# Weaving a layer's dependent attention steps between its dense products on TensorE

## The chip, the cores and the metric

The kernel runs on one core of one Trainium2 chip. The metric is the device time of one execution in microseconds (us); a smaller number is better. Three runs of the kernel before gave 2191.29, 2193.53 and 2195.86 us, so its median is 2193.53 us.

## The reference

One layer of a decoder trunk is computed for 512 positions of width 2048, all in float32. Three groups of heads read the same normed input, and their outputs are put side by side and go through one output projection; a SwiGLU network follows. Cut to what matters here:

```python
h = rmsnorm(x, norm1_g)
(u, v, dq, dk, dv, gq, gk, gv, gr, gcode) = jnp.split(h @ w_in, IN_SPLIT_IDX, axis=-1)
a_out = gmlp_mixer(u, v, ...)          # gelu(u) * (W_s layernorm(gelu(v)) + b), chunks of 128
b_out = diff_attention(dq, dk, dv, ...)  # 6 heads; (softmax(s1) - lam * softmax(s2)) @ v, then rmsnorm
c_out = gla_mixer(gq, gk, gv, gr, gcode, ...)  # 4 heads; gated linear attention, rmsnorm, * silu(r)
x = x + jnp.concatenate([a_out, b_out, c_out], -1) @ w_out
x = x + swiglu(rmsnorm(x, norm2_g), w_ffn_in, w_ffn_out)
return rmsnorm(x, final_g)
```

## The kernel before

Matrices lie in tiles of 128 partitions, and float32 products are made of three products of a reduced form: every operand is split into a high part (cast by ScalarE) and a low part (subtracted by VectorE), and `mm3` (L115) multiplies high by high, high by low and low by high. These are the dense products. Weights come in by DMA from SyncE's queue in halves of 128x1024 and are split by `split_w` (L105) or in `xstat` (L145).

The work around the change has this order in the program. First the value projection of the gMLP group (`xstat` "a") and the root mean square. Then the small spatial products `sp` (L262). Then the GLA values ("c", two blocks of columns), and the gate codes (`gct`, L287). Then 28 outputs of 128 columns each by `wstat` (L192): queries and keys of the four GLA heads (`wsg`), the gates (`wsr`), queries and keys of the six attention heads (`wsd`), and the gMLP's u (`wsu`). Each is 16 tiles deep, so 48 dense products of 512 columns. Between them stand the values of the differential attention ("b", L448: 384 products of 384 columns).

Two kinds of dependent chains hang on these. `gla(h, q, k)` (L309) takes a gate product `z`, three activations with different tables (L317 to L319), and then nine levels hs = 1, 2, 4, ... 256: exponentials on ScalarE (L356, L360), products on VectorE (L361, L362), four small matmuls `A` on TensorE (L341), a masked copy back (L343), and the running sums that the next level needs (L376, L378). Outputs `o` (L396), a norm, and transposes `ox` (L412) end a head. `attn(h)` (L453) makes stacked operands (L465 to L470), and for four blocks of queries scores `sc` (L481), softmax pieces, the difference of the two (L499 to L502) and transposes `pt` (L506); then `do` (L513), a norm, and transposes `dx` (L526).

Last, the gMLP gate (L537, L538) and the split of the mixed activations into `mxs` (L543 to L545) feed the output projection `wo_half` (L601). `mxs` takes the memory of `xs`, the split input, once the last `wstat` has read it. The output projection begins with the first half of the depth of four outputs (LEAD) and then takes their second halves.

Small matmuls and transposes share four PSUM banks (pool `sml`), dense products another four (`big`). The order of the instructions on each engine is not that of the program text: the compile's scheduler lets each engine take what it expects to be ready, by its own estimates, so on TensorE too the small steps stand where the scheduler put them.

Of the kernel before, what the change touches and what calls it, by code (L numbers as in the profile page):

```python
# [8 lines left out]
F32 = mybir.dt.float32  # L9
# [7 lines left out]
P = 128  # L17
# [32 lines left out]

@with_exitstack
def trunk_kernel(
# [22 lines left out]
    act, dve, pe, pool = nc.scalar, nc.vector, nc.tensor, nc.gpsimd  # L75
# [69 lines left out]
    def xstat(src, width, blocks, evac, name, first=False):  # L145
        for b, (c0, cw) in enumerate(blocks):
# [4 lines left out]
            for kn in steps:  # L151
# [40 lines left out]
    def wstat(j, name, halves=(0, 1)):  # L192
        b = big.tile([P, T], F32, tag="b", name=f"ws{name}")
        for hf in halves:
            wh, wl = split_w(wst[j, hf].rearrange("p k c -> p (k c)"), 1024, f"{name}_{hf}")
            for kk in range(8):
                k = 8 * hf + kk
# [61 lines left out]
    for g in range(4):  # L259
        pg = ps(f"sp{g}")  # L260
        for n in range(4):
            pe.matmul(pg[:, n * P:n * P + P], lhsT=va[:, n, g * P:g * P + P], rhs=spw[:, g], start=True, stop=True)  # L262
        dve.scalar_tensor_tensor(out=mix[:, g].rearrange("p (a b) -> p a b", b=P),
                                 in0=pg.rearrange("p (a b) -> p a b", b=P), scalar=lngs[:, g:g + 1],
                                 in1=spbb[:, g:g + 1].to_broadcast([P, 4, P]), op0=ALU.mult, op1=ALU.add)
# [19 lines left out]
    pt = ps("gct")  # L285
    for i in range(4):
        pe.transpose(pt[:16, i * P:i * P + P], gcs[:, i], ident)  # L287
    for r in (0, 32, 64):
        dve.tensor_copy(gcf[r:r + 16], pt[:16])
    act.copy(gct[:96], gcf[:96])  # L290
    dve.tensor_sub(gct[32:64], gcf[32:64], gct[32:64].bitcast(F32))
# [17 lines left out]
    def gla(h, q, k):  # L309
# [12 lines left out]
        dve.memset(suf, 0.0)  # L322

# [24 lines left out]
        hs = 1  # L348
        while hs <= 256:
# [12 lines left out]
            dve.tensor_mul(v(c)[:, :, 1], v(c)[:, :, 1], v(qh)[:, :, 1])  # L362
            if hs <= 64:
# [11 lines left out]
            if hs < 256:  # L375
                dve.tensor_add(v(suf)[:, :, 0], v(suf)[:, :, 0],  # L376
                               v(pre)[:, :, 1, hs - 1:hs].to_broadcast([DK, nb, hs]))
                dve.tensor_add(v(pre)[:, :, 1], v(pre)[:, :, 1],  # L378
                               v(pre)[:, :, 0, hs - 1:hs].to_broadcast([DK, nb, hs]))
            hs *= 2  # L380
        blk = {(0, 1): 4, (2, 3): 5, (0, 2): 6, (0, 3): 7, (1, 2): 8, (1, 3): 9}
# [46 lines left out]
    gla(3, *gq[3])  # L428

# [23 lines left out]
    def attn(h):  # L453
# [6 lines left out]
        q, k = qk  # L460
        quads = []
        for m in range(2):
            own, other = slice(64 * m, 64 * m + 64), slice(64 - 64 * m, 128 - 64 * m)
            qh, ql, kk = (stacked(f"{n}{h}_{m}") for n in ("qh", "ql", "kk"))
            act.copy(kk[own], k[own])  # L465
            dve.tensor_sub(kk[other], k[own], kk[own].bitcast(F32))
            for r in (own, other):
                act.copy(qh[r], q[own])
            for r in (own, other):
                dve.tensor_sub(ql[r], q[own], qh[own].bitcast(F32))  # L470
            quads.append((qh, ql, kk))
# [57 lines left out]
    for h in range(6):  # L529
        attn(h)  # L530
# [537 lines left out]
```

## Time and profile before

| | us |
|---|---|
| median of three runs | 2193.53 |
| the profiled execution, its own time | 2196.51 |
| its span, first to last instruction | 2194.7 |
| TensorE busy with matmuls (PE) | 2153.8 (98%) |
| VectorE busy (DVE) | 1522.8 (69%) |
| ScalarE busy (ACT) | 1010.5 (46%) |
| mean granted TensorE clock | 0.988 of full speed |

The page shows TensorE near full from end to end, so the few places where it is not are what is to be looked for. The granted clock is 1.00 (2.4 GHz) or 0.50 (1.2 GHz) at any moment; a stretch's mean below 1.00 says how much of it was at the lower level. A matmul's end is modelled, so a wait that is shorter than the modelled end doesn't show as idle time. A busy time alone therefore says less than the step from one start to the next.

### The profile page before, as it was taken

The numbers are of one execution on the slowest core, as the hardware profiler recorded it, in microseconds if no ns is written. First come the engines' busy times: TensorE is split into PE (matmuls) and PEld (weight loads), VectorE is DVE, ScalarE is ACT, GpSimd is POOL, SyncE is SP. The second block draws the span as 40 slices with busy tenths as digits, with TensorE's granted clock in tenths as the row PEclk, the third lists the DMA queues.
The fourth block names the chain that finished last, engine by engine and source line by source line (L and its number), as shares of the span: only waits on it lengthen the run. The fifth ranks groups of instructions, "written<-read, shape, count | busy, mean of one in ns | idle before, by whom it ended". The sixth has DMA issues, their size and how long they took to land.

```text
span 2194.7 us, 37812 instructions
## 1 busy us (share of the span) xinstructions
PE 2153.8 (98%) x15650; PEld 2053.9 (94%) x15650; DVE 1522.8 (69%) x2046; ACT 1010.5 (46%) x1456; POOL 58.7 (3%) x126
## 2 busy tenths in 40 slices
PE   9999999999989999999999999999999999999997
PEld 7988798878879999999999999999999999999987
DVE  6433754376665759777777777777777689888746
ACT  6323555355565546444444444444444634533444
POOL 1000000000001000000000000000000000000000
PEclk9999989999999999999999999999999999999998
DMA  6332121322237774343333333433333654733335
GB/s 204 90 106 96 34 58 46 104 77 77 70 129 240 226 229 160 123 148 117 140 119 133 130 129 117 149 119 122 114 130 119 199 154 141 229 113 103 111 102 179
DMA packets 105260, 284.63 MB, mean 130 GB/s; under 512 B 11216, under 2 KB 42368, under 8 KB 105088
## 3 DMA queue, kind: packets, MB, share of 16 engines
q1 hardware_dynamic: 81728, 236.88, 33.5%
q0 software_dynamic: 6720, 27.53, 3.4%
q10 hardware_dynamic: 16640, 17.80, 2.7%
q8 instruction: 123, 2.02, 0.4%
q14 instruction: 49, 0.40, 0.1%
HBM read 256.74 MB, written 25.43 MB: 129 GB/s over the span
## 4 chain that ended last, share of the span: by engine, by line
PE 93%; DVE 3%; ACT 2%; DMA 1%; issue 1%; SPq 0%; DVEq 0%; ACTq 0%
PE bx L116 7%; PE bx L118 7%; PE bx L117 7%; PE bz L117 4%; PE bz L118 4%; PE bz L116 4%; PE wo L116 3%; PE wo L117 3%; PE wo L118 3%; PE sx L118 2%; PE sx L116 2%; PE sx L117 2%; PE by L116 2%; PE by L118 2%; PE by L117 2%; PE wsd L116 2%
## 5 line engine op out<-in xcount | busy, mean ns | idle before, releaser
L118 PE MATMUL bx<-op,fl 128*128 128x256 f32 x1344 | 378.8, 282 | 0.4 <-DVE fl L659 0.4
L116 PE MATMUL bx<-op,fh 128*128 128x256 f32 x1344 | 379.1, 282 | 0.0
L117 PE MATMUL bx<-op,fh 128*128 128x256 f32 x1344 | 378.5, 282 | 0.0
L658 ACT CAST fh<-s 128x1024 fp32r<-128x1024 f32 x168 | 176.3, 1050 | 267.6 <-PE bx L117 127.1
L659 DVE TENSOR_TENSOR fl<-s,fh 128x1024 fp32r<-128x1024 f32 x168 | 205.4, 1223 | 87.3 <-ACT fh L658 85.2
L118 PEld LDWEIGHTS bx<-op,fl 128*128 128x128 f32 x1344 | 254.0, 189 | 0.6 <-DVE fl L659 0.6
L116 PEld LDWEIGHTS bx<-op,fh 128*128 128x128 f32 x1344 | 254.4, 189 | 0.0
L117 PEld LDWEIGHTS bx<-op,fh 128*128 128x128 f32 x1344 | 254.1, 189 | 0.0
L658 ACT CAST fh<-f 128x1024 fp32r<-128x1024 f32 x126 | 132.2, 1049 | 198.9 <-PE bx L117 72.3
L118 PE MATMUL bz<-op,fl 128*128 128x256 f32 x672 | 189.8, 282 | 0.1
L117 PE MATMUL bz<-op,fh 128*128 128x256 f32 x672 | 189.8, 282 | 0.0
L116 PE MATMUL bz<-op,fh 128*128 128x256 f32 x672 | 189.5, 282 | 0.0
L659 DVE TENSOR_TENSOR fl<-f,fh 128x1024 fp32r<-128x1024 f32 x126 | 154.0, 1222 | 35.0 <-ACT fh L658 35.0
L116 PE MATMUL wo<-mxs,wh_o 128*128 128x256 f32 x512 | 145.6, 284 | 0.0
L117 PE MATMUL wo<-mxs,wh_o 128*128 128x256 f32 x512 | 145.3, 284 | 0.0
L118 PE MATMUL wo<-mxs,wl_o 128*128 128x256 f32 x512 | 145.2, 284 | 0.0
L116 PE MATMUL sx<-fop,wh_s 128*128 128x256 f32 x448 | 127.1, 284 | 2.5 <-ACT wh_s L855 2.5
L118 PEld LDWEIGHTS bz<-op,fl 128*128 128x128 f32 x672 | 127.7, 190 | 0.3 <-DVE fl L659 0.3
L117 PEld LDWEIGHTS bz<-op,fh 128*128 128x128 f32 x672 | 127.8, 190 | 0.0
L116 PEld LDWEIGHTS bz<-op,fh 128*128 128x128 f32 x672 | 127.7, 190 | 0.0
L118 PE MATMUL sx<-fop,wl_s 128*128 128x256 f32 x448 | 127.2, 284 | 0.4 <-DVE wl_s L856 0.4
L117 PE MATMUL sx<-fop,wh_s 128*128 128x256 f32 x448 | 127.1, 284 | 0.0
(439 smaller groups left out, 5941.6 us busy)
## 6 DMA issues: line engine op xcount, KB each, us to landing
f<-wf SPq DMA_DIRECT2D x168, 512.0 KB, 3.8
w_o<-wout SPq DMA_DIRECT2D x32, 512.0 KB, 4.3
w2o<-wout SPq DMA_DIRECT2D x32, 512.0 KB, 4.6
sraw<-wf SPq DMA_DIRECT2D x32, 448.0 KB, 3.8
sw<-wf SPq DMA_DIRECT2D x32, 448.0 KB, 4.2
opd<-tmp POOLq DMA_DIRECT2D x14, 896.0 KB, 4.0
w_d<-wst SPq DMA_DIRECT2D x24, 512.0 KB, 3.3
w_g<-wst SPq DMA_DIRECT2D x16, 512.0 KB, 3.3
```

The costliest lines, as they stand in the source:

```text
L116: pe.matmul(out, lhsT=lh, rhs=rh, start=start, stop=False, skip_group_check=skip)
L117: pe.matmul(out, lhsT=lh, rhs=rl, start=False, stop=False, skip_group_check=skip)
L118: pe.matmul(out, lhsT=ll, rhs=rh, start=False, stop=stop, skip_group_check=skip)
L658: act.copy(wh, a)
L659: dve.tensor_sub(wl, a, wh.bitcast(F32))
```

## The change

TensorE's calls go through a small object `Queue`. It keeps a running estimate of TensorE time, and from the spatial products to the first half of the output projection every matmul is marked to stay in the order of the program. That order is now written by hand: the dependent chains (spatial products, gate codes, four GLA heads, six attention heads) are generators, and a `tick` ahead of each dense step of `mm3` runs those chains whose delay has passed; a `yield 3.4` asks, by that estimate, for 3.4 us of other TensorE work behind a step. The GLA level's factors are now made one level ahead of their product. The GLA heads follow one another from the gate outputs on (`wsr`) and no longer from the queries and keys of the third head. In the attention, the first probability is no longer scaled by its sum (the norm behind takes the sum in), and two of the stacked operands are copied by ScalarE instead of subtracted by VectorE. The gMLP gate, the split into `mxs` and the first halves of the output projection now stand behind the last `wsu` and inside the kept order.

```diff
+class Queue:
+
+
+
+    def __init__(self, tc):
+        self.tc, self.held, self.t, self.chains = tc, False, 0.0, []
...
+    def note(self, ins, out, rhs):
+        n = 1
+        for x in out.shape[1:]:
+            n *= x
+        self.t += max(0.112, 0.006 + n * 0.00044) if rhs.dtype == F32R else 2 * max(0.111, n * 0.00083)
+        if self.held:
+            self.tc.keep_in_program_order(ins)
...
+    def begin(self, chain, delay):
+        self.chains.append([chain, self.t + delay])
+
+    def tick(self, until=None):
+        for c in list(self.chains):
+            while c in self.chains and (until or self.t >= c[1]):
+                try:
+                    c[1] = self.t + next(c[0])
+                except StopIteration:
+                    self.chains.remove(c)
...
+    pe = Queue(tc)
...
         for hf in halves:
             wh, wl = split_w(wst[j, hf].rearrange("p k c -> p (k c)"), 1024, f"{name}_{hf}")
             for kk in range(8):
+                pe.tick()
                 k = 8 * hf + kk
                 c = slice(kk * P, kk * P + P)
...
+    def spatial():
+        for g in range(4):
+            pg = ps(f"sp{g}")
+            for n in range(4):
+                pe.matmul(pg[:, n * P:n * P + P], lhsT=va[:, n, g * P:g * P + P], rhs=spw[:, g], start=True, stop=True)
...
+            yield 2.0
+
+    pe.held = True
+    pe.begin(spatial(), 14.0)
...
+    pe.begin(codes(), 4.0)
...
+        def factors(hs):
...
+        c = factors(1)
+        yield 5.0
+        hs = 1
+        while hs <= 256:
+            nxt = factors(2 * hs) if hs < 256 else None
             if hs <= 64:
                 pick(c, hs, f"{h}_{hs}")
...
+            c = nxt
             hs *= 2
+            yield 3.4
+        far[0] = h + 1
+        while gated[0] < (4 if h < 2 else 6):
+            yield 1.0
...
-    gq = [gla_qk(0), gla_qk(1)]
+    gated = [0]
+
+    def silu(i0, i1):
+        act.activation(mix[:, MIXC + i0:MIXC + i1], mix[:, MIXC + i0:MIXC + i1], AF.Silu)
+        gated[0] = i1
+
+    def heads():
+        for h in range(4):
+            while len(gq) <= h or far[0] < h:
+                yield 1.0
+            pe.begin(gla(h, *gq[h]), 2.0)
+            yield 1.0
+
+    far = [0]
+    gq = [gla_qk(0)]
+    pe.begin(heads(), 0.0)
     for i in range(C_FULL):
         b = wstat(8 + i, f"r{i}")
         dve.tensor_mul(mix[:, MIXC + i], b, rs1)
-        act.activation(mix[:, MIXC + i], mix[:, MIXC + i], AF.Silu)
-    gla(0, *gq[0])
-    gq.append(gla_qk(2))
-    gla(1, *gq[1])
-    gq.append(gla_qk(3))
-    for i in range(C_FULL, 6):
-        act.activation(mix[:, MIXC + i], mix[:, MIXC + i], AF.Silu)
-    gla(2, *gq[2])
-    gla(3, *gq[3])
+    silu(0, C_FULL)
+    for h in range(1, 4):
+        gq.append(gla_qk(h))
+    silu(C_FULL, 6)
...
+            act.copy(qh[own], q[own])
             act.copy(kk[own], k[own])
+            dve.tensor_sub(ql[own], q[own], qh[own].bitcast(F32))
             dve.tensor_sub(kk[other], k[own], kk[own].bitcast(F32))
-            for r in (own, other):
-                act.copy(qh[r], q[own])
-            for r in (own, other):
-                dve.tensor_sub(ql[r], q[own], qh[own].bitcast(F32))
+            act.copy(qh[other], q[own])
+            act.copy(ql[other], ql[own].bitcast(F32))
             quads.append((qh, ql, kk))
+        yield 9.0
...
-            dve.reciprocal(st[:, 6:8], st[:, 4:6])
-            dve.tensor_mul(st[:, 7:8], st[:, 7:8], neglam)
-            dve.tensor_scalar_mul(pr[0][:, :w], pr[0][:, :w], st[:, 6:7])
+            dve.reciprocal(st[:, 6:7], den[:, 4 + qt:5 + qt])
+            dve.scalar_tensor_tensor(out=st[:, 7:8], in0=st[:, 6:7], scalar=neglam, in1=den[:, qt:qt + 1],
+                                     op0=ALU.mult, op1=ALU.mult)
...
+        p0, p1 = scores(0), scores(1)
+        yield 5.0
+        p2 = scores(2)
+        yield 4.0
+        turn(0, p0)
+        turn(1, p1)
+        yield 3.0
+        p3 = scores(3)
+        yield 3.0
+        turn(2, p2)
+        yield 5.0
+        turn(3, p3)
+        yield 2.0
...
+        dve.scalar_tensor_tensor(out=ds[:, 4:8], in0=den[:, 0:4], scalar=128 * EPS, in1=den[:, 0:4],
+                                 op0=ALU.mult, op1=ALU.mult)
+        dve.tensor_add(ds[:, 0:4], ds[:, 0:4], ds[:, 4:8])
+        act.activation(ds[:, 0:4], ds[:, 0:4], AF.Sqrt, scale=1.0 / 128)
         dve.reciprocal(ds[:, 4:8], ds[:, 0:4])
...
+        pe.begin(attn(h, *attn_qk(h)), 0.0)
...
+    ugs = []
     for g in range(4):
         b = wstat(24 + g, f"u{g}", (1, 0) if g == 3 else (0, 1))
-        ug = t2(f"ug{g}")
-        dve.tensor_mul(ug, b, rs1)
-        act.activation(ug, ug, AF.Gelu_apprx_tanh)
-        dve.tensor_mul(mix[:, g], mix[:, g], ug)
+        ugs.append(qk_tile(f"ug{g}"))
+        dve.tensor_mul(ugs[g], b, rs1)
+
+    def gate():
+        for g in range(4):
+            act.activation(ugs[g], ugs[g], AF.Gelu_apprx_tanh)
+            dve.tensor_mul(mix[:, g], mix[:, g], ugs[g])
 
 
     mxs = operand("mxs")
-    for k in ORDER:
-        hi, lo = (mxs[w][SLOT[k] // 4][:, SLOT[k] % 4] for w in range(2))
-        act.copy(hi, mix[:, k])
-        dve.tensor_sub(lo, mix[:, k], hi.bitcast(F32))
+
+    def split_mix(ks):
...
+    def wo_half(n, th, hf):
...
+    split_mix(ORDER[:11])
+    wo_half(0, 0, 0)
+    gate()
+    split_mix(ORDER[11:15])
+    for n in range(1, LEAD):
+        wo_half(n, 0, 0)
+    pe.drain()
+    pe.held = False
+    split_mix(ORDER[15:])
...
             if th == 0 and n == LEAD:
-                for m in range(LEAD):
-                    wo_half(m, 0, 0)
                 for m in range(LEAD):
                     wo_half(m, 0, 1)
```

On TensorE, between the second and the third level of GLA head 0, before (`A0_2`, `A0_4` are the levels' small products, `wsg20` a dense output):

```order
L341 MATMUL A0_2_1635<-c2_0_1630 128x64 x4
L116 MATMUL wsg20_1767<-xs02_103,wh_g20_1_1800 128x512
L117 MATMUL wsg20_1767<-xs12_107,wh_g20_1_1800 128x512
L118 MATMUL wsg20_1767<-xs02_103,wl_g20_1_1801 128x512
L116 MATMUL wsg20_1767<-xs03_104,wh_g20_1_1800 128x512
L117 MATMUL wsg20_1767<-xs13_108,wh_g20_1_1800 128x512
L118 MATMUL wsg20_1767<-xs03_104,wl_g20_1_1801 128x512
L341 MATMUL A0_4_1648<-c4_0_1643 128x64 x4
```

Six dense products stand there (5 to 10 between the other levels of this head). The same place in the changed kernel (`wsr1` is the dense output there; every matmul has the line of the helper):

```order
L67 MATMUL A0_2_1336<-c2_0_1296 128x64 x4
L67 MATMUL wsr1_1319<-xs00_101,wh_r1_0_1322 128x512
L67 MATMUL wsr1_1319<-xs10_105,wh_r1_0_1322 128x512
L67 MATMUL wsr1_1319<-xs00_101,wl_r1_0_1323 128x512
...
L67 MATMUL wsr1_1319<-xs01_102,wh_r1_0_1322 128x512
L67 MATMUL wsr1_1319<-xs11_106,wh_r1_0_1322 128x512
L67 MATMUL wsr1_1319<-xs01_102,wl_r1_0_1323 128x512
L67 MATMUL A0_4_1361<-c4_0_1329 128x64 x4
```

Twelve dense products stand between the two, and 12 to 18 between the levels of all four heads.

On TensorE, the end of the last attention head before (`pt5_3`, `do5`, `dx5` are its last steps, `wo0` the output projection):

```order
L116 MATMUL wsu3_4804<-xs01_102,wh_u3_0_4837 128x512
L117 MATMUL wsu3_4804<-xs11_106,wh_u3_0_4837 128x512
L118 MATMUL wsu3_4804<-xs01_102,wl_u3_0_4838 128x512
L506 MATMUL pt5_3_4578<-ident_510,p5_3_0_4570 128x128 x4
L513 MATMUL do5_4584<-dv_2540,dat5_4491 128x128 x10
L526 MATMUL dx5_4603<-ident_510,don5_4601 128x128 x4
L116 MATMUL wo0_0_4957<-mxs02_4871,wh_o0_00_4960 128x256
```

and in the changed kernel:

```order
L70 MATMUL pt5_3_4702<-ident_510,p5_3_0_4645 128x128 x4
L67 MATMUL wsu2_4692<-xs00_101,wh_u2_0_4695 128x512
...
L67 MATMUL do5_4714<-dv_2238,dat5_4516 128x128 x10
L67 MATMUL wsu2_4692<-xs00_101,wh_u2_0_4695 128x512
...
L70 MATMUL dx5_4762<-ident_510,don5_4733 128x128 x4
L67 MATMUL wsu2_4692<-xs02_103,wh_u2_1_4752 128x512
...
L67 MATMUL wo0_0_4881<-mxs02_4853,wh_o0_00_4884 128x256
```

Nothing dense stood between the three last steps; now 6 products stand ahead of `do5`, 21 ahead of `dx5`, and 66 (the rest of `wsu2` and all 48 of `wsu3`) between `dx5` and `wo0`.

On VectorE, the split of the mixed activations (`mxs1` tiles) in the changed kernel, beside the low parts of the output projection's weights (`wl_o`) and the gate of the last u (`ug3`):

```order
L622 TENSOR_TENSOR don5_4733<-do5_4714,ds5_4727 128x512
L150 TENSOR_TENSOR wl_u3_0_4822<-w_u3_0_4819,wh_u3_0_4821 128x1024
L638 TENSOR_TENSOR ug2_4786<-wsu2_4692,rs1_99 128x512
L150 TENSOR_TENSOR wl_o0_00_4885<-w_o0_00_4882,wh_o0_00_4884 128x1024
L643 TENSOR_TENSOR mix_79<-mix_79,ug2_4786 128x512
L652 TENSOR_TENSOR mxs12_4857<-mix_79,mxs02_4853 128x512 x4
L150 TENSOR_TENSOR wl_o1_00_4932<-w_o1_00_4929,wh_o1_00_4931 128x1024
L652 TENSOR_TENSOR mxs13_4858<-mix_79,mxs03_4854 128x512 x4
L652 TENSOR_TENSOR mxs10_4855<-mix_79,mxs00_4851 128x512 x2
L638 TENSOR_TENSOR ug3_4849<-wsu3_4788,rs1_99 128x512
L652 TENSOR_TENSOR mxs10_4855<-mix_79,mxs00_4851 128x512
L652 TENSOR_TENSOR mxs11_4856<-mix_79,mxs01_4852 128x512 x3
```

Before, eleven of these splits stood ahead of `don5`, in the last head's softmax; now all sixteen stand behind it.

## Rows read from the trace of the kernel before

**Rows 1.** Page, part 1: busy us and share of the span, by engine.
```profile
PE 2153.8 (98%) x15650; PEld 2053.9 (94%) x15650; DVE 1522.8 (69%) x2046; ACT 1010.5 (46%) x1456; POOL 58.7 (3%) x126
```

**Rows 2.** Windows: stretch, length, busy us by engine, clock, DMA share, GB/s.
```profile
120.00:215.00 95.00, 95.00 (x422) 77.91 (x422) 31.84 (x33) 24.95 (x28) 0.00 (x0) 1.00 0.30 99
215.00:295.00 80.00, 77.42 (x419) 65.24 (x418) 54.46 (x116) 47.40 (x92) 1.65 (x8) 0.98 0.17 50
295.00:375.00 80.00, 73.73 (x408) 70.33 (x407) 44.13 (x103) 42.80 (x90) 0.00 (x0) 0.87 0.15 43
440.00:620.00 180.00, 177.44 (x873) 144.30 (x872) 123.63 (x262) 101.20 (x198) 0.00 (x0) 1.00 0.23 77
620.00:637.00 17.00, 8.07 (x39) 7.42 (x38) 9.89 (x20) 9.80 (x17) 0.00 (x0) 0.71 0.10 31
```

**Rows 3.** Waits of TensorE, 0 to 660 us: us in total, times, longest.
```profile
PE pt L506 <- DVE p L502: 7.8, 6, 5.6
PE A L341 <- DVE c L362: 7.0, 5, 2.6
PE dx L526 <- DVE don L522: 3.3, 1, 3.3
```

**Rows 4.** Chain of waits, the gate codes: start us, us, what.
```profile
124.56 0.44 PE gct L287 x4
```

**Rows 5.** Timeline of TensorE, 272 to 276 us: start, us, instruction, count.
```profile
272.34 1.00 PE L341 MATMUL A<-c 96*128 96x64 f32 x8
273.15 0.48 PE L117 MATMUL wsg<-xs,wh_g 128*128 128x512 f32 x1
273.47 0.39 PE L118 MATMUL wsg<-xs,wl_g 128*128 128x512 f32 x1
...
275.09 0.39 PE L116 MATMUL wsg<-xs,wh_g 128*128 128x512 f32 x1
```

**Rows 6.** Timeline of TensorE, 298 to 306 us; in brackets idle before, releaser.
```profile
297.72 0.34 PE L169 MATMUL b<-wh_b,xs 128*128 128x384 f32 x1
...
298.77 0.34 PE L169 MATMUL b<-wh_b,xs 128*128 128x384 f32 x1
298.95 0.33 PE L170 MATMUL b<-wl_b,xs 128*128 128x384 f32 x1
301.02 1.08 PE L341 MATMUL A<-c 96*128 96x64 f32 x8 [1.74 <-DVE c L362]
301.90 0.42 PE L171 MATMUL b<-wh_b,xs 128*128 128x384 f32 x1
```

**Rows 7.** Timeline of ScalarE, 213 to 224 us, head 0 of GLA.
```profile
214.08 1.05 ACT L111 CAST wh_g<-w_g 128x1024 fp32r<-128x1024 f32 x1 [4.52 <-PE wsr L117]
215.03 0.68 ACT L317 ACTIVATE ab<-z,gbs 96x512 f32<-96x512 f32 x1
215.61 0.62 ACT L420 ACTIVATE mix<-mix 128x512 f32<-128x512 f32 x1
216.25 1.28 ACT L318 ACT_TABLE_LOAD   x1
217.54 0.64 ACT L318 ACTIVATE ab<-ab 96x512 f32<-96x512 f32 x1
```

**Rows 8.** Chain of waits, 210 to 245 us: first, fourth and fifth levels of head 0.
```profile
222.46 1.11 PE A L341 x8
...
231.85 0.84 PE A L341 x8
...
234.15 0.84 PE A L341 x8
```

**Rows 9.** Timeline, 618 to 637 us: the tail, TensorE and VectorE.
```profile
621.77 1.23 DVE L112 TENSOR_TENSOR wl_o<-w_o,wh_o 128x1024 fp32r<-128x1024 f32 x1 [0.32 <-ACT wh_o L111]
622.99 1.89 DVE L545 TENSOR_TENSOR mxs<-mix,mxs 128x512 fp32r<-128x512 f32 x3
626.47 1.09 PE L506 MATMUL pt<-ident,p 128*128 128x128 f32 x4 [5.62 <-DVE p L502]
634.62 1.11 PE L526 MATMUL dx<-ident,don 128*128 128x128 f32 x4 [3.31 <-DVE don L522]
635.39 0.56 PE L116 MATMUL wo<-mxs,wh_o 128*128 128x256 f32 x1
```

More of the change, by code (lines that the diff above doesn't have):

```diff
@@ L48, in group_of, with matmul, transpose, drain @@
     return 0 if S0 <= j < S0 + 14 else 1 if S1 <= j < S1 + 14 else None
+class Queue:
[8 more added lines that the diff above has]
+            self.tc.keep_in_program_order(ins)
+    def matmul(self, out, lhsT, rhs, **k):
+        self.note(self.tc.nc.tensor.matmul(out, lhsT=lhsT, rhs=rhs, **k), out, rhs)
+    def transpose(self, out, in_, ident):
+        self.note(self.tc.nc.tensor.transpose(out, in_, ident), out, in_)
+    def begin(self, chain, delay):
[7 more added lines that the diff above has]
+                    self.chains.remove(c)
+    def drain(self):
+        while self.chains:
+            self.tick(True)
 @with_exitstack
@@ L258, in trunk_kernel @@
     dve.memset(one1, 1.0)
[L259 to L265, printed above, removed]
+    def spatial():
[3 more added lines that the diff above has]
+                pe.matmul(pg[:, n * P:n * P + P], lhsT=va[:, n, g * P:g * P + P], rhs=spw[:, g], start=True, stop=True)
+            dve.scalar_tensor_tensor(out=mix[:, g].rearrange("p (a b) -> p a b", b=P),
+                                     in0=pg.rearrange("p (a b) -> p a b", b=P), scalar=lngs[:, g:g + 1],
+                                     in1=spbb[:, g:g + 1].to_broadcast([P, 4, P]), op0=ALU.mult, op1=ALU.add)
+            yield 2.0
+    pe.held = True
+    pe.begin(spatial(), 14.0)
     gv = mix[:, 4:10].rearrange("p a t -> p (a t)").rearrange("p (i c) -> p i c", c=768)
@@ L284, in trunk_kernel, with codes @@
     dve.memset(gcf[:96], 0.0)
[L285 to L291, printed above, removed]
+    def codes():
+        pt = ps("gct")
+        for i in range(4):
+            pe.transpose(pt[:16, i * P:i * P + P], gcs[:, i], ident)
+        for r in (0, 32, 64):
+            dve.tensor_copy(gcf[r:r + 16], pt[:16])
+        act.copy(gct[:96], gcf[:96])
+        dve.tensor_sub(gct[32:64], gcf[32:64], gct[32:64].bitcast(F32))
+        yield 0.0
+    pe.begin(codes(), 4.0)
     def qk_tile(name):
@@ L459, in attn @@
             qk.append(t)
-        q, k = qk
+        return qk
+    def attn(h, q, k):
         quads = []
@@ L529, in trunk_kernel @@
     for h in range(6):
-        attn(h)
+        pe.begin(attn(h, *attn_qk(h)), 0.0)
+    ugs = []
     for g in range(4):
         b = wstat(24 + g, f"u{g}", (1, 0) if g == 3 else (0, 1))
-        ug = t2(f"ug{g}")
-        dve.tensor_mul(ug, b, rs1)
-        act.activation(ug, ug, AF.Gelu_apprx_tanh)
-        dve.tensor_mul(mix[:, g], mix[:, g], ug)
-    mxs = operand("mxs")
-    for k in ORDER:
-        hi, lo = (mxs[w][SLOT[k] // 4][:, SLOT[k] % 4] for w in range(2))
-        act.copy(hi, mix[:, k])
-        dve.tensor_sub(lo, mix[:, k], hi.bitcast(F32))
+        ugs.append(qk_tile(f"ug{g}"))
[4 more added lines that the diff above has]
+            dve.tensor_mul(mix[:, g], mix[:, g], ugs[g])
+    mxs = operand("mxs")
+    def split_mix(ks):
+        for k in ks:
+            hi, lo = (mxs[w][SLOT[k] // 4][:, SLOT[k] % 4] for w in range(2))
+            act.copy(hi, mix[:, k])
+            dve.tensor_sub(lo, mix[:, k], hi.bitcast(F32))
+    wob, wqs = {}, []
+    HALF = (slice(0, TH), slice(TH, T))
+    def wo_half(n, th, hf):
+        hs = HALF[th]
+        if hf == 0:
+            wob[n] = big.tile([P, T], F32, tag="b", name=f"wo{n}_{th}")[:, :TH]
+        wh, wl = split_w(wout[n, hf].rearrange("p k c -> p (k c)"), 1024, f"o{n}_{th}{hf}",
+                         None if hf == 0 or pe.held else wqs[0].tile([P, 1024], F32, tag="raw", bufs=3, name=f"w2o{n}_{th}"))
+        for kk in range(8):
+            pe.tick()
+            i = 8 * hf + kk
+            k = SLOT[ORDER[i]]
+            c = slice(kk * P, kk * P + P)
+            mm3(wob[n], wh[:, c], wl[:, c], mxs[0][k // 4][:, k % 4, hs], mxs[1][k // 4][:, k % 4, hs],
+                i == 0, i == KT - 1)
+    split_mix(ORDER[:11])
[7 more added lines that the diff above has]
+    split_mix(ORDER[15:])
     mp.release()
@@ L598, in trunk_kernel @@
              9: lambda: op_pair(2, b21)}
-    wob, xrs = {}, {}
-    def wo_half(n, th, hf):
-        hs = HALF[th]
-        if hf == 0:
-            wob[n] = big.tile([P, T], F32, tag="b", name=f"wo{n}_{th}")[:, :TH]
-        wh, wl = split_w(wout[n, hf].rearrange("p k c -> p (k c)"), 1024, f"o{n}_{th}{hf}",
-                         None if hf == 0 else wq.tile([P, 1024], F32, tag="raw", bufs=3, name=f"w2o{n}_{th}"))
-        for kk in range(8):
-            i = 8 * hf + kk
-            k = SLOT[ORDER[i]]
-            c = slice(kk * P, kk * P + P)
-            mm3(wob[n], wh[:, c], wl[:, c], mxs[0][k // 4][:, k % 4, hs], mxs[1][k // 4][:, k % 4, hs],
-                i == 0, i == KT - 1)
     def wo_out(n, th):
```

34 lines of the change are left out of this document (20 added, 14 removed).

## The prediction

> **What bounds the kernel now.** I read the page first: TensorE is busy for 2153.8 of 2194.7 us [rows 1], so only a stretch in which it waits or runs at the lower clock can give time back. Then the windows over the part that the change touches [rows 2]. From 120 to 215 us there is nothing to get: 95.00 busy of 95.00, clock 1.00. The GLA heads' 160 us (215 to 375) have 2.6 + 6.3 = 8.9 us idle and a clock of 0.98 and 0.87, that is 1.6 + 10.4 = 12 us of capacity gone at 1.2 GHz. The attention (440 to 620) is idle for 2.6 of 180. The tail (620 to 637) is the worst: 8.9 of 17 idle, clock 0.71, so another 4.9. Idle and slow together make some 37 us. The waits say on what [rows 3]: a transpose for the softmax, a level's product for its factors, the last transposes for the norm, all of them VectorE results at the end of a dependent chain.
>
> A busy time hides short waits, so I set the stage's work against its length. It runs from the gate codes at 124.56 [rows 4] to the first product of the output projection at 635.39 [rows 9]: 510.8 us. One 512-column product takes 0.231: seven steps from 273.47 to 275.09 [rows 5]. There are 28 x 48 = 1344 of them, 311 us. One of 384 columns takes 0.175, six steps from 297.72 to 298.77 [rows 6]; 384 make 67. The small instructions: eight A take 0.81 [rows 5], so 0.10 to 0.11 each up to 128 columns, and 512 of that kind (256 in the GLA levels and their diagonal, 16 at 128 columns included in 272, then 120 `do`, 116 transposes, 4 codes) make 54; 196 wider ones (`o`, `sc`, the last levels, `z`) at 0.17, my estimate between 0.10 and 0.23, make 33. The sum is 465, and the stage loses 510.8 - 465 = 45 us. That is the most the change can give, since it takes no matmul away.
>
> **The change, part by part.** *What stays.* TensorE has the same matmuls in the same forms, and from the first `wo0` product on they come in the order of before. All of it is decided in the stage of 511 us.
>
> *The tail* stands from 626.47 - 5.62 = 620.85 to 635.39 [rows 9], 14.5 us, with 3 us of work in it (four transposes, twenty `do`, four `dx` at 0.105 to 0.11): 11.5 of the 45. Now 6 products stand ahead of `do5` and 21 ahead of `dx5`, 21 x 0.231 = 4.9 us. The norm between the two made TensorE wait for 3.31 us [rows 9], table load included, so it is hidden. What is late next is the split into `mxs`: before, eleven of sixteen ran inside the last softmax; now all follow the norm and wait for `xs`, whose last reader is `wsu3`. On VectorE that is 16 x 0.63 + four weight halves at 1.23 [rows 9] + about four 0.6 products = 17.4 us. The cover from the middle of `wsu3` (the first tiles come free there) to the second halves of the output projection is 5.5 + 4 x 24 x 0.119 = 17 us (a 256-column step taken as half of 0.231 and a little). So VectorE is just full. The first splits are done in time, since the first half of each output needs only eight of them; the third output's low weights stand behind eight splits and the gate, and I make them 0.5 to 1 us late. I take 1; with a VectorE that enters this part 4 us late it is 5.
>
> *The GLA heads and the attention* hold the other 33.5. Of these 21 show as idle or slow under the GLA heads and 2.6 under the attention (above); the hidden 10 I halve between them, an estimate: 26 and 7.5.
>
> *The GLA heads.* Each level's product followed the last by 2.05 to 2.3 us (231.85 to 234.15) [rows 8], which is what the chain of sums, exponentials and products needs, with 5 to 10 products as cover; any late step showed at once, and the clock fell after. Now 12 to 18 products stand there: 12 x 0.231 + 0.81 = 3.6 us, or 15 x 0.175 + 0.81 = 3.4 under "b", 1.1 to 1.3 us more than the chain. One weight split (1.23 [rows 9]) fits into that, and the factors are one level ahead. Each head's start is tighter. From `ab` to the first product took 222.46 - 215.03 = 7.4 [rows 7, 8], with a Silu (0.62) that has moved; so 6.8, plus 0.2 from `z` to ScalarE, plus a weight cast (1.05 [rows 7]) which heads 0 and 1 now have in between: 8.0. Cover: 30 products and the diagonal, 6.9 + 0.8 = 7.7. Late by 0.3, twice. Under head 2 a Silu over two tiles with two table loads stands between levels 4 and 8: 2 x 1.28 + 1.1 = 3.7 against three levels' slack of 3.4, late by 0.3. Head 3 shares ScalarE with the four copies that empty the banks of "b", late by 0.7. With 0.5 per head for what I can't see, 3.6; I take 4.
>
> A row speaks on the table loads: the activation after one starts 0.01 us behind it (216.25 + 1.28 to 217.54) [rows 7]. The Trainium skill (ScalarE: Activation LUTs, "What ACT_TABLE_LOAD costs") counts for every switch, besides the load, a drain of about 1.38 us. No drain shows on this ScalarE, so the trace does not agree. By that rule three loads per head start would be 4.1 us longer for four heads, some 16 us less gain, an estimate from that page; by the row nothing.
>
> *The attention.* VectorE loses the scaling of the first probability (24 instructions) and 12 subtractions, ScalarE gets 12 copies and 4 table loads. Both have room (VectorE 124 of 180, ScalarE 101 of 180 [rows 2]). With about 96 products per head, 22 us, between the steps of two heads, I take 0.7 per head as still lost, over half of what it is now: 4.
>
> *Sum.* 1 + 4 + 4 = 9 of the 45 stay; 36 go. The profiled execution's own 2196.5 becomes 2160.5. The median shown is 3.0 below that execution, so I forecast 2158 us. Unknown from both sides: at best all 45 go (2149); at worst every late step named comes at double and the tail at 5 (-27, 2167).
>
> **The rivals.**
>
> *One order, many stops.* A late step now holds back everything. That it does so is in the trace: at 298.95 `b` products stop, the A at 301.02 waits 1.74 us, and the next `b` product, which needs none of it, runs only behind it [rows 6]. The Trainium skill (TensorE: Matmul & The Clock Gate, "Step-by-step: what each phase is for") says that matmuls stay in program order and only weight loads are pulled ahead; the trace agrees, by those 1.74 us. The written order has some 108 places where a dependent step stands in front of dense work (4 spatial, 1 codes, 48 GLA, 55 attention). 45 / 108 = 0.42 us late at each is the point from which nothing is gained; at 0.6 it is 65 - 45 = 20 slower, 2213. For it: delays come from an estimate, and a wait here measured up to 2.6 [rows 3]. Against: the slack of 1.1 to 1.3 per level above, and that before only 12 waits of these kinds showed [rows 3] with half the cover.
>
> *The GLA's start stays the bound.* ScalarE's queue, not TensorE's order, could set z to first level and the Silu of head 2. If each head is still 3 us late in all and the clock falls after it, 12 of the 26 stay: 2158 + 12 = 2170. For it: 0.87 of the clock sits exactly there. Against: 7.7 of cover to 8.0.
>
> *Dearer table loads.* If a load among more work costs double its 1.28 us [rows 7], three at each head's start are 4 x 3 x 1.28 = 15 us late: 2173. Against: nothing follows the one load in rows 7.
>
> *The splits take the tail's place.* VectorE is full for 17 us; if it comes in late, the first output projection waits 9 to 10 instead of 1: 2167.
>
> *Nothing changes.* If the scheduler's order was already limited by VectorE throughput, waits only move: 2193. Against: VectorE is busy for 0.55 to 0.69 of these windows [rows 2].
>
> **How the numbers follow.** Forecast 0.73 (its own range 2149 to 2167); GLA start 0.11; table loads 0.02; splits 0.06; nothing 0.03; one order 0.05. The measurement of this kernel can tell about 0.2%, 4.4 us. Faster: 0.73 + 0.11 + 0.02 + 0.06 = 0.92; same 0.03; slower 0.05. The range of 8 in 10 reaches from all 45, less 2 for the spread of single runs, to a GLA that stays half late with the table loads: 2147 to 2174.
>
> **What would show it.** Right: the stretch from the gate codes to the first `wo0` product lasts some 475 us instead of 511; the granted clock is 1.00 in all windows between; TensorE's waits for level factors and for `dx` are gone from the list or under 1 us each; level products stand 3.4 to 3.6 us apart. Wrong: a wait of over 1 us at one place in every head; a clock under 1.00 between 215 and 620 us; `wo0` to `wo3` waiting for a split or its weights.

## The result, and the profile after

The changed kernel takes 2169.36 us (median of four runs, 2168.35 to 2170.79), the kernel before 2193.66 beside it; the ratio is 0.989 with an interval of 0.987 to 0.991. It is faster, by 24 us by the medians and by 27.2 by the two profiled executions (2196.51 and 2169.28). The forecast was 36 and 2158 us. 2169 lies inside the range of 2147 to 2174, but above the forecast's own 2149 to 2167.

On the page of the changed kernel TensorE has the same 15650 products as in [rows 1] and is busy 18 us less for them:

```profile
PE 2135.5 (99%) x15650; PEld 2042.0 (94%) x15650; DVE 1507.3 (70%) x2022; ACT 1020.2 (47%) x1468; POOL 58.8 (3%) x126
```

Its windows, with the columns of [rows 2]:

```profile
120.00:215.00 95.00, 92.08 (x437) 76.55 (x436) 42.37 (x72) 38.66 (x61) 0.71 (x3) 0.98 0.25 83
215.00:295.00 80.00, 77.90 (x391) 64.60 (x390) 44.92 (x83) 36.06 (x61) 0.94 (x5) 1.00 0.21 65
295.00:375.00 80.00, 78.40 (x489) 77.14 (x488) 45.59 (x98) 40.68 (x78) 0.00 (x0) 1.00 0.25 75
440.00:600.00 160.00, 157.59 (x805) 131.74 (x804) 101.20 (x225) 102.33 (x195) 0.00 (x0) 1.00 0.22 73
600.00:615.00 15.00, 15.00 (x89) 13.18 (x88) 13.70 (x21) 13.12 (x22) 0.00 (x0) 1.00 0.24 81
```

The window over 295 to 375 us, 0.87 of the clock before, has 1.00 (products at the lower clock are busy for longer, so the page's 18 us), and the last row, over the end of the stage (609.32), is full. But the first window, where there was nothing to get before, is now 2.9 us idle at 0.98: the GLA heads begin earlier, and something in them waits. TensorE's waits over the stage (total, times, longest) say what:

```profile
PE o L67 <- ACT og L461: 6.0, 8, 2.0
PE do L67 <- ACT dat L591: 2.4, 4, 0.6
PE wo L67 <- DVE wl_o L150: 1.2, 1, 1.2
PE A L67 <- DVE c L413: 1.1, 2, 0.9
```

None of the three waits of [rows 3] is left at its size: `pt` and `dx` are gone, `A` has 1.1 of 7.0. In their place stand names that the list of before did not have at all: `o`, `do` and `wo`. The largest wait, 6.0 us, is at `o`, the output products of the GLA heads: eight waits, two in each head. In time, TensorE at head 0 (start, us, instruction, count; in brackets idle before and releaser):

```profile
200.86 0.49 PE L67 MATMUL o<-mix,at 128*128 128x192 f32 x2
202.25 1.89 PE L67 MATMUL o<-mix,at 128*128 128x192 f32 x10 [0.91 <-ACT og L461]
206.09 1.89 PE L67 MATMUL o<-mix,at 128*128 128x192 f32 x8 [1.95 <-ACT og L461]
207.53 1.31 PE L67 MATMUL wsg<-xs,wh_g 128*128 128x512 f32 x2
```

and ScalarE there:

```profile
200.83 1.05 ACT L149 CAST wh_g<-w_g 128x1024 fp32r<-128x1024 f32 x1 [4.52 <-PE wsr L67]
201.78 0.32 ACT L461 ACTIVATE og<-o 128x192 f32<-128x192 f32 x1
...
202.21 1.28 ACT L483 ACT_TABLE_LOAD   x1
203.51 1.91 ACT L483 ACTIVATE mix<-mix 128x2048 f32<-128x2048 f32 x1
205.32 0.31 ACT L461 ACTIVATE og<-o 128x192 f32<-128x192 f32 x1
...
205.63 0.32 ACT L461 ACTIVATE og<-o 128x192 f32<-128x192 f32 x1
```

A head's outputs lie in two PSUM banks of two pieces each (2 + 4 and 6 + 8 instructions), and ScalarE squares each piece (`og`). In this program the second piece of a bank starts only when ScalarE has read the first, though the columns differ. At head 0 a cast stands ahead of the first square (0.91 us of waiting); the output gate's table load and Silu, 1.28 + 1.91, and one more square stand ahead of the one at 205.63, for which the last eight products wait 1.95. The other three heads wait about 0.5 twice. The Trainium skill (PSUM — Partial Sum Buffer, "PSUM bank collisions raise a hardware error") says that the compiler makes instructions of two engines on one bank (and the same 32 partitions) depend on one another, reads and writes alike, by bank and not by address; the eight waits agree, and the prediction did not draw on that page. No run here shows what the chip does without that dependency.

The kernel before had the same two steps and no wait, because its scheduler put dense products into each gap, two into the first and three into the second. Its TensorE at head 0:

```profile
243.42 0.49 PE L396 MATMUL o<-mix,at 128*128 128x192 f32 x2
243.61 0.53 PE L117 MATMUL wsg<-xs,wh_g 128*128 128x512 f32 x1
...
244.26 1.89 PE L396 MATMUL o<-mix,at 128*128 128x192 f32 x10
245.85 0.53 PE L116 MATMUL wsg<-xs,wh_g 128*128 128x512 f32 x1
...
246.68 1.54 PE L396 MATMUL o<-mix,at 128*128 128x192 f32 x8
```

The next, 2.4 us, is at `do`: in four attention heads the last eight products wait 0.6 us each for the copy of the last transposes, which on ScalarE stands behind casts of the next head's operands.

To size these, I set each TensorE step of the stage against the usual step of its kind, as the prediction did for the whole stage. Between 120 us and the first `wo` product the kernel before is 44.3 us over (45 in the prediction), the changed one 18.1. Of the 18.1, 8.3 lie between two `o` products (the 6.0 of waits and slow steps behind them), 3.5 between two `do`, 1.4 ahead of a first level, and some 5, the rest, in hundredths over the dense products. By the same steps the 45 of the kernel before lie as the prediction split them: some 26 under the GLA heads, 7 in the attention and 12 in the tail. The first `wo` product comes at 609.32 instead of 635.39 [rows 9], 26.1 earlier.

### The profile page after: what moved, and what is told of

Same layout as the page of the kernel before. It is cut to its first block, busy times and chain, and to the rows that moved or that the text cites. A ratio compares the mean times of both kernels' runs of the same rounds, so it can differ in the third digit from the quotient of the medians.

```text
span 2167.5 us, 37807 instructions
## 1 busy us (share of the span) xinstructions
PE 2135.5 (99%) x15650; PEld 2042.0 (94%) x15650; DVE 1507.3 (70%) x2022; ACT 1020.2 (47%) x1468; POOL 58.8 (3%) x126
## 4 chain that ended last, share of the span: by engine, by line
PE 93%; ACT 3%; DMA 2%; DVE 1%; issue 1%; SPq 0%; DVEq 0%; ACTq 0%
PE bx L67 22%; PE bz L67 11%; PE wo L67 8%; PE sx L67 7%; PE wsd L67 6%; PE by L67 6%; PE sz L67 4%; PE wsg L67 3%; PE fb_None L67 3%; PE b L67 3%; PE c L67 3%; PE rb L67 3%; PE wsu L67 2%; PE sy L67 2%; PE a L67 2%; PE wsr L67 2%
## 5 line engine op out<-in xcount | busy, mean ns | idle before, releaser
L67 PE MATMUL bx<-op,fh 128*128 128x256 f32 x2688 | 485.3, 282 | 0.0
L67 PEld LDWEIGHTS bx<-op,fh 128*128 128x128 f32 x2688 | 414.2, 189 | 0.0
L67 PE MATMUL bz<-op,fh 128*128 128x256 f32 x1344 | 244.2, 282 | 0.0
L67 PE MATMUL wo<-mxs,wh_o 128*128 128x256 f32 x1024 | 182.9, 282 | 0.0
L67 PEld LDWEIGHTS wo<-mxs,wh_o 128*128 128x128 f32 x1024 | 157.3, 188 | 0.1
L67 PEld LDWEIGHTS sx<-fop,wh_s 128*128 128x128 f32 x896 | 139.1, 191 | 2.9 <-ACT wh_s L971 2.9
L67 PE MATMUL wsd<-xs,wh_d 128*128 128x512 f32 x384 | 122.2, 399 | 0.0
L67 PE MATMUL by<-op,fh 128*128 128x256 f32 x672 | 122.2, 282 | 0.0
L67 PEld LDWEIGHTS by<-op,fh 128*128 128x128 f32 x672 | 104.3, 190 | 0.0
L67 PEld LDWEIGHTS wo<-mxs,wl_o 128*128 128x128 f32 x512 | 96.5, 188 | 1.6 <-DVE wl_o L150 1.6
```

Of the source, the lines that this page charges most:

```text
L67: self.note(self.tc.nc.tensor.matmul(out, lhsT=lhsT, rhs=rhs, **k), out, rhs)
```

## The experiments

Twelve kernels ran in four sets, each set beside the kernel before; its median was 2196.78, 2195.23, 2194.13 and 2191.82 us in the sets. Between sets the ratio is what compares. The last column is the start of the first `wo` product in the trace, the end of the stage.

| kernel | us | ratio, interval | first `wo` |
|---|---|---|---|
| changed | 2169.36 | 0.989 (0.987–0.991) | 609.32 |
| e1 no marks | 2161.05 | 0.984 (0.981–0.986) | 600.59 |
| e2 marks to the attention | 2166.45 | 0.986 (0.984–0.989) | 608.65 |
| e3 marks from the attention | 2161.47 | 0.984 (0.982–0.986) | 601.59 |
| e4 outputs in turn, with a gap | 2169.60 | 0.987 (0.985–0.990) | 612.52 |
| e5 outputs unmarked | 2165.36 | 0.987 (0.986–0.989) | 605.52 |
| e6 shorter gaps | 2174.53 | 0.991 (0.990–0.993) | 616.98 |
| e7 bare tail | 2188.90 | 0.997 (0.996–0.998) | 629.43 |
| e8 arithmetic only | 2190.02 | 0.997 (0.996–0.999) | 618.36 |
| e9 outputs in turn, Silu behind | 2160.16 | 0.985 (0.982–0.988) | 600.18 |
| e10 no gaps | 2207.07 | 1.006 (1.004–1.008) | 642.77 |
| e11 no marks, wider piece at `do` | 2159.45 | 0.985 (0.982–0.987) | 598.34 |
| e12 e9 with that wider piece | 2156.53 | 0.984 (0.982–0.987) | 598.34 |

**Set 1: is it the kept order that gives the gain?** e1 takes the marks away and leaves the program text as the change wrote it; e2 and e3 mark one half of the stage each; e4 first tried to cure `o`.

```diff
-    pe.held = True
```

> The changed kernel with no matmul marked: the program text stays woven, the scheduler alone orders TensorE. Theory (the kept order is what holds dense products back as cover): the scheduler takes dependent steps as early as it thinks them ready, the level products stand close again, the clock falls under the GLA heads and the tail is bare: 2185 to 2192 us. Rival (the woven text is enough, since the scheduler follows the text): 2168 to 2172 us.

> Marked from the spatial products to the last values of the attention, not beyond: the GLA heads keep the written order, the attention and the tail are the scheduler's. Theory (the tail's 11 us came back through the kept order): dense products are spent ahead of the last head again and the tail waits 8 to 11 us: 2177 to 2181 us. Rival (the attention and the tail gained from the other edits, the shorter VectorE work and the late gate): 2169 to 2171 us.

> Marked only from the attention on: the GLA heads are the scheduler's. Theory (GLA gave about 14 of the 24 us): 2181 to 2186 us, with clock below 1.00 between 215 and 375 us. Rival (GLA heads gain nothing from the order, their loss only moved to the output products): 2169 to 2172 us.

My theory fell in all three, and the times came in below the rivals' ranges too. Without any mark the kernel is 8 us faster than with them. The scheduler follows the woven text by itself (30, 30, 24 and 42 dense products between a head's `z` and its first level, as in the changed kernel); and at `o` it does what it did before. TensorE of e1 at head 0:

```profile
200.38 2.31 PE L67 MATMUL o<-mix,at 128*128 128x192 f32 x12
202.39 0.76 PE L67 MATMUL wsg<-xs,wh_g 128*128 128x512 f32 x2
...
205.79 1.46 PE L67 MATMUL o<-mix,at 128*128 128x192 f32 x8
```

It starts both banks, then runs dense products while the Silu runs, then the rest. e2 and e3 put the cost of the marks into the GLA: marked there alone, the waits at `o` are 6.0 as in the changed kernel and the stage ends at 608.65; marked from the attention on, there is none and the time is that of e1.

e4 filled the two banks in turn, with a piece of dense work between the halves (`yield 1.4`), the Silu left where it was.

> Each GLA head's output products alternate between their two banks, and 1.4 us of dense work stands between the first and the second half. Theory (the 8 us that I had not forecast are TensorE waiting until ScalarE has read the bank it is to write next): the waits of o for og go from 6 us to under 1, and the time to 2161 to 2164 us. Rival (o waits for ScalarE's queue as a whole, Silu and weight casts, and the wait only moves to the next step): 2167 to 2170 us.

The time is the rival's, and so is most of the mechanism: `o` waits once (2.1 us, the Silu of head 0), but its head chain is now longer, and the first levels of later heads wait, 5.2 us in three places. One of them, on TensorE, right behind the last transposes of head 1:

```profile
287.38 1.03 PE L70 MATMUL ox<-ident,og 128*128 128x128 f32 x8
290.97 1.32 PE L67 MATMUL A<-c 96*128 96x64 f32 x8 [2.56 <-DVE c L413]
```

**Set 2: the outputs, the gaps, the tail, the arithmetic.** e5 unmarks only the `o` products.

```diff
+            pe.held = False
             for e in range(2):
...
+            pe.held = True
```

> The changed kernel with one step unmarked: the GLA heads' output products (80 of TensorE's instructions) are left to the scheduler, all else keeps the written order. Theory (the gain comes from the woven text; the mark costs where a kept order runs into a bank that ScalarE still reads, and that is the o step, 8.3 us over its steps): the waits of o for og are gone and the time is that of the kernel with no marks, 2159 to 2163 us beside 2196 for before on this chip (ratio 0.983 to 0.985). Rival (what the unmarked kernel gained lies all over the stage, in single products that move forward by one or two places): 2166 to 2170.

About half of it came, and the time, 2165.4, lies between the two ranges: 4.6 us of waits are left, 2.9 of them at the Silu. That the dense products around, still marked, can't move in would explain it; it was not shown. e6 makes the gaps between the levels shorter.

```diff
-            yield 3.4
+            yield 1.6
```

> The changed kernel with 1.6 instead of 3.4 us asked for between two GLA levels, order kept. Theory (12 to 18 products as cover are what took the level waits away): with 6 or so products a level follows the last by about 2.0 us, under the chain's 2.05 to 2.3, so each of 32 levels is 0.2 to 0.5 late, the waits of A for c are 6 to 15 us, the clock falls: 2176 to 2186 us. Rival (the cover is not what counts, but that the factors are made one level ahead and the weights' splits stand elsewhere): within 2 us of the changed kernel.

The theory fell at the levels. Six products stand between them, about as many as before and half of the changed kernel's, and the levels follow one another by 2.3 us:

```profile
160.45 1.00 PE L67 MATMUL A<-c 96*128 96x64 f32 x8
...
162.73 1.00 PE L67 MATMUL A<-c 96*128 96x64 f32 x8
```

The waits at `A` are 1.9 us in all, and 1.2 of these stand at the heads' first levels, 0.7 between levels. So 12 to 18 products are more cover than a level needs. The 5 us were lost elsewhere: the waits at `o` are 8.3 us instead of 6.0 (longest 3.4), and the clock of the window from 120 to 215 us is 0.95 where the changed kernel has 0.98. e10 went to no products at all. e7 writes the last dense outputs (`wsu`) without ticks, so that the last attention steps stand bare behind them.

> The changed kernel with nothing woven into the products of u: the steps of the attention that are left then run behind them, with no dense products between. Theory (the tail's gain is the cover of u): most of a head's chain is bare, 12 us as before and up to 20 more, with the clock down: 2181 to 2200 us. Rival (the tail is hidden by the late splits and the gate anyway): under 2175 us.

As expected, 2188.9. The window around its tail, and what TensorE waits for there:

```profile
600.00:640.00 40.00, 24.70 (x139) 22.71 (x139) 19.39 (x47) 18.72 (x38) 0.00 (x0) 0.70 0.22 74
```

```profile
PE dx L70 <- DVE don L623: 7.7, 2, 4.5
PE pt L70 <- DVE p L582: 4.0, 1, 4.0
PE pt L70 <- ACT p L576: 3.6, 2, 3.0
```

15 us idle, and 0.70 of the clock: the dense `wsu` products between the last steps are worth 20 us. e8 is the kernel before with only the new arithmetic of the attention.

> The kernel before with only the attention's arithmetic of the change: no scaling of the first probability, the sum taken into the norm, two stacked operands copied by ScalarE. Order and scheduler as before. Theory (VectorE was not the bound in the attention): within 3 us of before, ratio 0.998 to 1.001. Rival (the shorter softmax chain is what the attention and the tail gained): 5 to 10 us faster, ratio 0.995 to 0.998.

2190.0, the rival's range: the arithmetic alone gives some 5 us. The waits for the softmax shrink and `wo` waits for its weights instead, while the GLA's waits are untouched:

```profile
PE A L341 <- DVE c L362: 7.0, 5, 2.6
PE wo L116 <- ACT wh_o L111: 5.0, 2, 3.8
PE pt L507 <- DVE p L503: 1.7, 4, 0.5
```

It does more than the 5 us say. With the shorter chain, the scheduler by itself puts 17 `wsu` products between the last head's `do` and `dx`, and both waits of the tail are gone:

```profile
617.77 0.40 PE L118 MATMUL wsu<-xs,wl_u 128*128 128x512 f32 x1
618.01 0.60 PE L530 MATMUL dx<-ident,don 128*128 128x128 f32 x4
618.36 0.36 PE L116 MATMUL wo<-mxs,wh_o 128*128 128x256 f32 x1
```

The first `wo` product comes 17.0 us earlier than before. About 5 of these stand already under the GLA heads, where this one execution (2184.64 us, the median is 2190.02) had a higher clock with the same waits; 12 lie in the attention and the tail, and 5.0 are given back where `wo` waits for its weights.

**Set 3: take the wait away, not the marks.** e9 keeps every mark, fills the banks in turn with nothing between, and starts the Silu behind the squares.

```diff
-        while gated[0] < (4 if h < 2 else 6):
-            yield 1.0
...
-        for u in range(2):
-            po = ps(f"o{h}_{u}")
-            for e in range(2):
+        for e in range(2):
+            for u in range(2):
+                po = pos[u]
...
         yield 9.0
+        while gated[0] < (4 if h < 2 else 6):
+            yield 1.0
```

> The changed kernel with its order still kept, but the two accumulators of a GLA head's output products are filled in turn (piece 0 of bank 0, piece 0 of bank 1, then piece 1 of each), and the wait for the output gate's projection stands behind a stretch of dense products, so that the gate's 1.9 us Silu and its 1.3 us table load do not stand between the two squares of head 0. Theory (what the kept order costs is that the second piece of a bank must wait until ScalarE has squared the first, and at head 0 for the Silu too): waits of o for the square fall from 6.0 us to under 1.5, the time goes to about 2162, the level of the kernel without marks (2161.1). Rival (the loss only moves on to the next dependent step, as it did when the outputs alternated with a dense product between them, 2169.6): waits of the first level products for their coefficients appear, 2167 to 2171.

2160.2, 9 us less than the changed kernel, with all marks. The twenty products of head 0 run in one piece, and so do those of the other three heads:

```profile
191.24 3.54 PE L67 MATMUL o<-mix,at 128*128 128x192 f32 x20
```

ScalarE's first three squares fall between, at 191.76, 192.73 and 193.38, one bank being read while the other is filled:

```profile
192.73 0.33 ACT L460 ACTIVATE og<-o 128x192 f32<-128x192 f32 x1 [0.55 <-PE o L67]
```

No wait of `o` is left in the list. So the wait at `o` is what the marks cost. e9 changes the turn and the Silu's place together; what each is worth alone was not tried. e10 takes the dense products from between the levels.

```diff
-            yield 3.4
+            yield 0.6
```

> The changed kernel with its order kept, and no dense product between the eight levels of the intra-chunk matrix of each GLA head (the pieces of 3.4 us become 0.6, which hands out none); the dense products of these gaps come at the heads' later places and at the end of the batch. Theory (each level's TensorE product waits for the chain mask, scale, VectorE, ScalarE of its own level, about 2.05 to 2.3 us, less 0.8 that the level's own products take): some 28 of the 32 levels wait 1.3 to 1.5 us, so 35 to 45 us more in the GLA stretch, waits of A for c of 35 us or more, the granted clock below 0.95 there, 2205 to 2220 us. Rival (the levels before one another are prepared ahead, so that the gaps were never needed): waits of A below 10 us and under 2185 us.

2207.1, slower than the kernel before, and in the time expected, but not in the way expected. Head 2 of e10 on TensorE:

```profile
296.46 1.08 PE L67 MATMUL A<-c 96*128 96x64 f32 x8
297.80 1.08 PE L67 MATMUL A<-c 96*128 96x64 f32 x8 [0.26 <-DVE c L413]
299.27 1.10 PE L67 MATMUL A<-c 96*128 96x64 f32 x8 [0.39 <-DVE c L413]
301.59 6.99 PE L67 MATMUL A<-c 96*128 96x64 f32 x32 [1.22 <-DVE c L413]
```

and three of its windows:

```profile
120.00:215.00 95.00, 90.06 (x403) 74.52 (x401) 42.00 (x71) 34.88 (x51) 0.00 (x0) 0.93 0.25 82
215.00:295.00 80.00, 76.13 (x353) 63.53 (x354) 38.30 (x74) 36.81 (x64) 1.65 (x8) 0.91 0.16 50
295.00:375.00 80.00, 72.31 (x368) 65.65 (x367) 43.83 (x102) 38.98 (x82) 0.00 (x0) 0.85 0.13 35
```

Without cover the levels come 1.34, 1.47 and 2.32 us apart. The waits at `A` are 9.2 us in 19 places, not 35. After the first three of this head the clock falls to 1.2 GHz (1.00 up to 302 us, 0.50 at 308 to 312), the 32 products of four levels take 6.99 us (0.22 each, twice the 0.10 of [rows 5]), and at that pace the factors, made a level ahead, keep up. Idle time in these windows is 16.5 against 6.6 us in the changed kernel, capacity lost to the clock 0.07 x 95 + 0.09 x 80 + 0.15 x 80 = 25.9 against 1.9: together 34, and the first `wo` product is 33.4 later.

e11 takes e1 and widens the dense piece ahead of `do`.

```diff
-        yield 2.0
+        yield 3.4
         po = ps(f"do{h}")
```

> The changed kernel without marks on any matmul, and the dense piece ahead of the dense attention's last output products widened from 2.0 to 3.4 us. Theory (those products wait 0.6 us in each of four heads for ScalarE's copy of the last transposed block): the waits of do for dat fall from 2.4 us (1.5 in the unmarked kernel) to 0, and the time is 1 to 2 us below the unmarked kernel's 2161.1, so 2159 to 2160. Rival (the products spent there are missing later in the batch, or the scheduler puts them elsewhere): 2161 or more.

The wait at `do` is gone and the stage ends 2.2 us before that of e1; the 1.6 us in the medians is within the runs' spread, and the ratio is no lower than that of e1.

**The best of both.** e12 is e9 with the wider piece.

> The changed kernel with its order kept and both cures: the two accumulators of a GLA head's outputs filled in turn with the Silu moved behind them, and the dense piece ahead of the dense attention's last output products widened from 2.0 to 3.4 us. Theory (the two losses stand at different places and add): no waits of o for the square and none of do for the copy, 2 us below the 2160.2 us of the first cure alone, so 2157.5 to 2159, and level with the unmarked kernel with the wider piece (2159.45), which means that the kept order by itself then costs nothing. Rival (the pieces spent ahead of do are missing at the tail, where wo then waits longer for its split weights): 2160 or more, with a wait of wo for wl_o above 3 us.

2156.5, the lowest median of all; but it ran beside a faster kernel before, and its ratio, 0.984, is that of e1 and e3, so no gain over these can be told. Its waits:

```profile
PE wo L67 <- DVE wl_o L150: 2.0, 2, 1.1
PE sc L67 <- ACT p L575: 1.1, 1, 1.1
PE A L67 <- DVE c L413: 0.9, 1, 0.9
```

Its stage ends at 598.34 like that of e11: with both cures the marks cost nothing that these runs can tell. They gain nothing either.

## Why the prediction was right, and where its size was off

- **The range.** 2169 is outside the forecast's own 2149 to 2167 and inside 2147 to 2174 only because that upper end allowed for late GLA heads and dearer table loads, neither of which came; that part is luck. Between the profiled executions 2160.5 was forecast and 2169.3 came, 8.8 us more. Two sums also do not hold: taken at its word, the worst case (both 4s doubled, the tail at 5) leaves 21 and gives 24, so 2169.5 and not 2167; and "GLA's start stays bound" adds 12 us to a forecast in which 4 of these already stay, so it stood for 2166 and not 2170.
- **What bounds the kernel** (45 us of the stage, 36 to be had): right. e12, with the same products, starts `wo` 37.1 us before the kernel before. The changed kernel got 26.1 of this.
- **The tail** (11.5, 1 left): right in size. `wsu` runs until the first `wo` product and `dx` waits for nothing. The third output's low weights, which the step made 0.5 to 1 late, come in time. `wo` does wait once, but 30.6 us behind its first product, at its 243rd, which belongs to the sixth output:

```profile
639.91 0.39 PE L67 MATMUL wo<-mxs,wl_o 128*128 128x256 f32 x1 [1.20 <-DVE wl_o L150]
```

The cause was told too narrowly. The step counted the products of the written order alone; e8 shows that the cheaper arithmetic, left to the scheduler, empties the tail as well, and loses 5.0 us at `wo`'s weights for it. e7 shows that there must be cover; 20 us is more than the 11.5, since with none at all the last two heads stop, too.
- **The GLA heads** (26, 4 left): this is the term that was mis-sized. The levels came as forecast: they stand 3.5 to 3.7 us apart (161.39 to 165.08 in head 0, 296.50 to 300.02 in head 2) and wait for nothing, except the first ones of heads 1 and 2, 1.4 us together. What failed is "With 0.5 per head for what I can't see, 3.6; I take 4": I went through the starts and the levels of a head and left out its end. The two halves of a bank, 8 places, measured 8.3, and the term 9.7.
- **Why the GLA's waits went** was wrong in part. The step put it down to 12 to 18 products between levels. But of the 7.9 us that TensorE waited for level factors before, 6.9 stand at the heads' first levels, at 301.02 [rows 6] and here:

```profile
222.46 1.11 PE L341 MATMUL A<-c 96*128 96x64 f32 x8 [1.76 <-DVE c L362]
261.20 1.08 PE L341 MATMUL A<-c 96*128 96x64 f32 x8 [0.81 <-DVE c L362]
343.12 1.23 PE L341 MATMUL A<-c 96*128 96x64 f32 x8 [2.55 <-DVE c L362]
```

Later levels waited 0.17 and 0.94, in the last head. The 2.05 to 2.3 us of [rows 8] are the five or six products in between (6 x 0.231 + 0.81 = 2.2) and not what the chain needs, and e6 has such gaps and hardly a wait in them; e10 shows only that no gap at all is too little. From `z` to the first level takes about as long as before (8.3 to 9.4 us beside 7.9 to 9.8), but more dense products cover it in three heads: 30, 30, 24 and 42 instead of 23, 25, 37 and 23. So, by these rows, the gain came at the starts of the heads, and with them the clock, which before fell behind such a wait (1.00 up to 301 us, 0.50 from 303 to 306). What each edit at the starts is worth was not tried.
- **The attention** (7.5, 4 left): right in size, at a place not named: 3.5 at `do`, behind the copies that the change gives to ScalarE and the casts.
- **Some 5 us** of the 45 lie spread over the dense products; they are in e12 as well (its stage is 6.6 over in all), so no order tried here gives them back.
- **One order, many stops** was given 0.05 for a slower kernel. Its mechanism is what cost the 8.3: a late product holds back dense products that do not need it, in eight waits at `o` (and four at `do`), where the prediction counted 108 places. Its price was wrong for nearly all others, as the levels show. The proof that I drew for it from [rows 6] was of a queue that runs in order; what it missed is that before, the scheduler chose the order and put cover at `o`. The Trainium skill (TensorE: Matmul & The Clock Gate, "Step-by-step: what each phase is for") has matmuls in program order; the trace agrees, since at 207.53 `wsg` products that need nothing of `o` run only behind it, and it is the program order itself that e1 changes.
- **GLA's start stays bound**: no. The clock is 1.00 from 215 on. The time given for it, 2170, came out, for another reason: luck of that sum.
- **Dearer table loads**: no. Silu starts 0.02 us behind its load (202.21 + 1.28 to 203.51). The Trainium skill's drain of 1.38 us per load (ScalarE: Activation LUTs, "What ACT_TABLE_LOAD costs") does not show here either.
- **Splits take the tail's place**, **nothing changes**: no; the last window is full, and the stage is 26.1 us shorter.
- Of the signs named, the stretch (480.8 us with 18 products, 4.2 us, moved ahead of its start, so 485 against 475), the clock in the first window (0.98; the sign asked for 1.00) and the wait over 1 us told of the miss, although that wait came at one head and not in every one.

## What to carry to other kernels

Weaving dependent steps between dense products in the program text, together with the edits that came with it, gives the gain (e1; the attention's arithmetic alone gave 5 us of it); pinning that order gives nothing more and takes away the scheduler's freedom at the steps that were not thought of. Who pins an order has to go through every dependent step, the two halves of one PSUM bank with a reader between them included, and either fill the banks in turn or put work there. Read the list of waits after such a change for names that the list before did not have: a step that was covered for free is not in it.

## What the runs showed of the hardware that was not expected

A stretch can lose more to the clock than to the waits that pull it down: in e10, 9.2 us of waits at the levels go with 24 us of capacity lost at 1.2 GHz beyond the changed kernel's. And in that state the waits leave the list: four levels, 32 products, ran in 6.99 us without a stop that the trace shows, where at 0.10 a product they would have waited for their factors, as the levels just before did.

The same waits can also go with another clock. In e8 TensorE's waits at `A` are those of the kernel before, 7.0 us in five places, longest 2.6, and the granted clock from 295 to 375 us is 0.94 where it was 0.87. The first level of head 3 starts at 338.25 instead of 343.12, so the clock alone made 5 us between these two executions.
